# Hybrid conformer and latent-attention trunk on one core: rotary tables made with both parts of the angle side by side, in fewer and wider steps that start sooner

## The chip, the cores and the metric

The kernel runs on one core of one Trainium2 chip. The metric is device time in microseconds (us). A core has TensorE (PE in the profile; its weight loads are PEld), VectorE (DVE), ScalarE (ACT), GpSimd (POOL) and SyncE (SP, which here only issues DMAs). Each engine works through its own list of instructions in order, and waits at an instruction until what it needs is there.

## The reference

Two layers. Each normalises x (256 positions, 2048 channels), multiplies it with one wide input weight, and splits the product into a convolution branch (GLU, causal depthwise convolution of width 31, LayerNorm over channels, SiLU, times a SiLU gate) and an attention branch. Both are projected, merged by sigmoid gates, projected once more and added to x.

```python
def rope_tables(positions, dtype):
    inv_freq = ROPE_THETA ** (-jnp.arange(0, QK_ROPE, 2, dtype=jnp.float32) / QK_ROPE)
    ang = positions.astype(jnp.float32)[..., None] * inv_freq
    cos = jnp.cos(ang)[:, :, None, :].astype(dtype)
    sin = jnp.sin(ang)[:, :, None, :].astype(dtype)
    return cos, sin

def hybrid_layer(...):
    proj = rmsnorm(x, norm_g) @ w_in
    ...
    y_conv = conv_branch(c_a, c_glu, c_gate, conv_w, conv_b, conv_ln_g, conv_ln_b) @ w_proj_conv
    y_mla = mla_branch(q_down, kv_down, k_pe, m_gate, cos, sin, ...) @ w_proj_mla
    y = jax.nn.sigmoid(g_conv) * y_conv + jax.nn.sigmoid(g_mla) * y_mla
    return x + y @ w_out
```

The positions go up to 1279, so an angle is up to some two hundred revolutions. The kernel reduces it to a fraction of one revolution before it takes the sine.

## The kernel before

**Products in parts.** Every fp32 weight is streamed in pieces of 256 rows (two groups of 128) by 512, 384 or 320 columns, numbered in the order of use (raw0, raw1, ...). ScalarE casts a piece to its high part (hi), VectorE subtracts to get the low part (lo), and TensorE adds three products for each group and each half of the positions: twelve matmuls a piece. hi is made three pieces ahead and lo two pieces ahead. A raw buffer (there are five) is free for the next load when both parts are made; there are four hi and three lo buffers, freed by TensorE.

**The order.** It is written out when the program is built, by a small planner. A slot is one weight piece. `product` (with `split_hi` and `split_lo`) lays down the splits and the matmuls of a piece, and `background` then does what is due in that slot: `at_slot(ahead, f, vec, act)` puts a job so many slots ahead and charges its estimated VectorE and ScalarE time to a budget. Each slot gives a budget, less the splits; a debt is carried on, what is left over is not:

```python
            budget[e] = min(budget[e], 0.0) + slot - split_us
```

While VectorE's budget is positive, the planner takes jobs from the list `fill`: the 31 taps of each of the eight convolution blocks, and behind them the LayerNorm, the gates and what makes the input of the projection. A tap is either an addition of what ScalarE scaled (`tap`) or a fused multiply-add (`v_t<-u_t,cst,v_t`). If VectorE's budget is spent elsewhere, the fills move to later slots. Classes around each engine (`InOrder`) then hold every engine to this order.

**The convolution's way to its projection.** In layer 0 the products are, in this order: GLU block 0 (pieces 0 to 7), three blocks of down projections (8 to 31), GLU and attention blocks, gates, and at the end gconv (pieces 244 to 275), pconv (276 to 307), the projection of the convolution branch, and wout. `layernorm` makes the mean (`mu`) and the variance (`var`) with two small matmuls each, which TensorE's order holds between two pieces. Then `apply` normalises each block, ScalarE takes the SiLU, `gated` multiplies by a gate that was parked in DRAM and comes back through POOL's queue as `turned`, and `separated` splits two blocks into the high part ycT0 (ScalarE) and the low part ycT1 (VectorE). There are four such groups; pconv reads the first with pieces 276 and 277, the second with 278 and 279, the third with 280 and 281 and the fourth with 282 and 283. If a group isn't laid down by then, `before_pconv` runs the fills until it is.

**The rotary tables.** `rope_tables` is a generator; each `next` lays down one step. The first loads the inverse frequencies and the positions, the third makes the angle and splits it into a part `ah` with few bits and the rest `al`. The number of revolutions is the angle times 1/(2 pi), which is cut into six pieces of 12 bits. For each piece and each part, `reduce_to` multiplies, rounds by adding and taking away 1.5 x 2^23, and subtracts; the fractions are added up in `turn`. Two more steps make sine and cosine, which the attention of both layers uses, the first time for the key's rotary part some slots behind the down projections.

The first GLU product is read by ScalarE and VectorE (`glu_evac`, the operations `su`) out of two PSUM banks; blocks of products take two pairs of banks in turn, so that down block 1 (from piece 16 on) writes these banks again.

Of the kernel before, what the change touches and what calls it, by code (L numbers as in the profile page):

```python
# [11 lines left out]
F32 = mybir.dt.float32  # L12
F32R = mybir.dt.float32r
I32 = mybir.dt.int32
AF = mybir.ActivationFunctionType
ALU = mybir.AluOpType
# [3 lines left out]
P = 128  # L20
T = 2
# [9 lines left out]
HALF = ROPE // 2  # L31
# [40 lines left out]
def revolution_pieces():  # L72

    from fractions import Fraction

    pi = Fraction(
        "3.14159265358979323846264338327950288419716939937510582097494459230781640628620899"
    )
    rest, out = 1 / (2 * pi), []
    for i in range(REVOLUTION_PIECES):  # L80
        unit = Fraction(1, 1 << (12 * (i + 1)))
        n = int(rest / unit)
        out.append(float(n * unit))
        rest -= n * unit
    return out
# [30 lines left out]
def trunk(ctx: ExitStack, tc: tile.TileContext, xT, x, g_in, pos, win, wuq, wukv, wpc, wpm, wo, cst, rows, invf, out):  # L116
# [19 lines left out]
    pe, vec, act, gps, sp = (InOrder(e) for e in (nc.tensor, nc.vector, nc.scalar, nc.gpsimd, nc.sync))  # L136
# [7 lines left out]
    work = pool("work", 1)  # L144
# [80 lines left out]
    def at_slot(ahead, f, vec=0.0, act=0.0, first=False):  # L225
        steps.insert(0 if first else len(steps), (clock[0] + ahead, (vec, act), f))
# [140 lines left out]
    def stat_of(hi, lo):  # L367
        return lambda k, t: (hi[:, k, t * P : (t + 1) * P], lo[:, k, t * P : (t + 1) * P])
# [120 lines left out]
    def rope_tables():  # L489

        invf_t = const.tile([P, HALF], F32, name="invf_t")
        sp.dma_start(invf_t, invf.partition_broadcast(P))
        pos_t = const.tile([P, T], I32, name="pos_t")
        sp.dma_start(pos_t, pos)
        yield
        yield
        posf = const.tile([P, T], F32, name="posf")
        vec.tensor_copy(posf, pos_t)
        tables = work.tile([P, 6, T, HALF], F32, tag="pr", name="tables")
        ang, ah, al, turn, whole, frac = (tables[:, i] for i in range(6))  # L500
        ah = ah.bitcast(F32R)
        for t in range(T):
            vec.tensor_scalar(ang[:, t, :], invf_t, posf[:, t : t + 1], None, op0=ALU.mult)
        vec.tensor_copy(ah, ang)
        vec.tensor_sub(al, ang, ah.bitcast(F32))
        yield
        big_half = 1.5 * 2.0**23

        def reduce_to(dst, src, scale):

            vec.tensor_scalar(whole, src, scale, big_half, op0=ALU.mult, op1=ALU.add)
            vec.tensor_scalar(whole, whole, -big_half, None, op0=ALU.add)
            vec.scalar_tensor_tensor(dst, src, scale, whole, op0=ALU.mult, op1=ALU.subtract)

        first = True
        for piece in revolution_pieces():
            for a in (ah.bitcast(F32), al):
                reduce_to(turn if first else frac, a, piece)
                if not first:
                    vec.tensor_add(turn, turn, frac)  # L520
                first = False
                yield
        for dst, shift in ((sin2, 0.0), (cos2, 0.25)):
            vec.tensor_scalar(frac, turn, shift, None, op0=ALU.add)
            reduce_to(ang, frac, 1.0)
            for h in range(2):
                act.activation(dst[:, :, h, :], ang, AF.Sin, scale=2.0 * np.pi)
            yield
            yield
# [24 lines left out]
    def first_sums(t, c):  # L554

        xts = []

        def begin():
            for a in (c, c + 1):
                xts.append(wide_p.tile([P, 512], F32, tag="w", name="xres"))  # L560
                sp.dma_start(xts[-1], x[t, :, a * 512 : (a + 1) * 512])

        def end():
            for a, xt in zip((c, c + 1), xts):
                junk = work.tile([P, 512], F32, tag="junk", name="junk")
                act.activation(junk, xt, AF.Square, accum_out=ss_x[:, t, a : a + 1])

        return begin, end


    for l in range(DEPTH):
# [22 lines left out]
        def down_evac(i, t, ps, down=down):  # L594
            at, n = DOWN_BLOCKS[i]
            act.activation(down[:, t, at : at + n], ps, AF.Copy, scale=rinv_x[:, t : t + 1])
# [108 lines left out]
        def rope_squares(b, part_of=part_of):  # L705
            sq = work.tile([P, T, 2, 2, HALF], F32, tag="qa", name="sq")
            act.activation(sq, part_of(b, "qr"), AF.Square)
            late.append(lambda: vec.tensor_reduce(part_of(b, "ss")[:, 2], sq.rearrange("p t a h c -> p t h a c"), axis=AX.XY, op=ALU.add))
# [575 lines left out]
        for kind, i, pl in planned:  # L1284
            if kind == "glu":
                at = EVAC_AT
                if i == 0 and l == 0:
                    at = 6
                    for n, (t, c) in enumerate([(0, 0), (0, 2), (1, 0), (1, 2)]):
                        begin, end = first_sums(t, c)  # L1290
                        at_slot((4, 5, 6, 9)[n], begin)
                        at_slot((9, 9, 10, 12)[n], end, 0.0, 1.5)
                    at_slot(13, sum_x, 2.2)
                elif i == 0:
                    at_slot(8, sum_x, 2.2)
                if i == 0:
                    at_slot(10, load_consts)
                product(pl, uses_h, lambda t, ps, i=i: glu_evac(i, t, ps), at, (0.9, 2.2), tardy=6 if i == 0 and l else None)
            elif kind == "down":
                if l == 0 and i == 0:  # L1300
                    tables = rope_tables()
                    for a in range(20):
                        at_slot(a + (2 if a < 2 else 7), lambda: next(tables, None), 0.0 if a < 2 else 0.95)
                product(pl, uses_h, lambda t, ps, i=i: down_evac(i, t, ps), costs=(0.0, 1.0))
                if i == len(DOWN_BLOCKS) - 1:
                    down_after()
            elif kind == "uq":
                if i == 0:
                    attention_tiles()
                product(pl, of_down(0), lambda t, ps, i=i: uq_evac(i, t, ps), costs=(0.0, 2.5))  # L1310
                if i % 3 == 0:
                    at_slot(EVAC_AT + 1, lambda i=i: rotate_q(4 * (i // 3)), 1.2)
            elif kind == "ukv":
                product(pl, of_down(4), lambda t, ps, i=i: ukv_evac(i, t, ps), costs=(0.0, 2.6))
                attention(i)
                d = 2 * (i // 4)
                if i % 4 < 3:
                    at_slot(3 + d, lambda i=i: rope_squares(i + 1), 0.4, 0.4)
                if i % 4 < 2:
                    at_slot(6 + d, lambda i=i: rotate_q(i + 1), 1.2)  # L1320
                elif i % 4 == 2:
                    at_slot(6 + d, lambda i=i: waiting_in(i + 1), 0.0, 1.6)
                    at_slot(7 + d, lambda i=i: rotate_q(i + 1), 1.2)
                if i == NPAIR - 1:
                    layernorm()
            elif kind == "mgate":
                product(pl, uses_h, lambda t, ps, i=i: mgate_evac(i, t, ps), costs=(0.0, 3.5))
            elif kind == "gmla":
                product(pl, uses_h, lambda t, ps, i=i: gmla_evac(i, t, ps), costs=(0.0, 2.7))
            elif kind == "pmla":  # L1330
                product(pl, stat_of(*keep["o"]), lambda t, ps, i=i: pmla_evac(i, t, ps), costs=(1.25, 0.0))
            elif kind == "gconv":
                product(pl, uses_h, lambda t, ps, i=i: gconv_evac(i, t, ps), costs=(0.0, 3.9))
            elif kind == "cgate":
                product(pl, uses_h, lambda t, ps, i=i: cgate_evac(i, t, ps), costs=(0.0, 2.0))
            elif kind == "pconv":
                while "yc" not in keep:
                    run_fill()
                product(pl, stat_of(*keep["yc"]), lambda t, ps, i=i: pconv_evac(i, t, ps), 0 if i == 3 else EVAC_AT, (2.4, 0.0),
                        before=before_pconv if i == 0 else None)  # L1340
            else:
                wout_begin(i)
                if last_layer and i == 3:
                    wout_end(pl, stat_of(*keep["y"]))
                    continue
                product(pl, stat_of(*keep["y"]), lambda t, ps, i=i, f=wout_evac: f(i, t, ps),
                        0 if i == 3 else EVAC_AT, (1.25, 1.5), tardy=6 if i == 0 else None)
# [108 lines left out]
```

## Time and profile before

| what | value |
|---|---|
| device time, median of 3 runs | 1884.52 us (1883.84 to 1885.91) |
| the profiled execution's own time | 1884.47 us |
| its span in the profile | 1882.7 us |
| mean granted TensorE clock | 0.999 |
| busy TensorE / VectorE / ScalarE / POOL | 99% / 84% / 72% / 26% |
| read from HBM | 399.18 MB |

A row of the chain or of a timeline has the start, the duration, engine, line, operation, output<-inputs and, in brackets, the idle time before it and what ended it. All instructions are issued by one helper, so all have line 127, and the names tell them apart. In a row of waits the numbers are the total, the count and the longest. A row by windows gives the stretch, its length, the busy time of PE, PEld, DVE, ACT and POOL with counts, the granted clock, the DMA share and GB/s. A row of one tile's instructions gives the count, then the shortest, median and longest duration in ns. A row of DMA issues gives the count, the size of one and the median time to landing.

### The profile page before, as it was taken

The numbers are of one execution on the slowest core, as the hardware profiler recorded it, in microseconds if no ns is written. First come the engines' busy times: TensorE is split into PE (matmuls) and PEld (weight loads), VectorE is DVE, ScalarE is ACT, GpSimd is POOL, SyncE is SP. The second block draws the span as 40 slices with busy tenths as digits, with TensorE's granted clock in tenths as the row PEclk, the third lists the DMA queues.
The fourth block names the chain that finished last, engine by engine and source line by source line (L and its number), as shares of the span: only waits on it lengthen the run. The fifth ranks groups of instructions, "written<-read, shape, count | busy, mean of one in ns | idle before, by whom it ended". The sixth has DMA issues, their size and how long they took to land.

```text
span 1882.7 us, 27123 instructions
## 1 busy us (share of the span) xinstructions
PE 1872.1 (99%) x8577; PEld 1571.8 (83%) x8577; DVE 1582.8 (84%) x2452; ACT 1361.7 (72%) x2456; POOL 493.0 (26%) x942
## 2 busy tenths in 40 slices
PE   9999999999999999899999999999999999999999
PEld 8988888888888888788889888888888888888887
DVE  6899998899999988766669899889899999885664
ACT  7678888888887875644557588788889878574442
POOL 1055555532200000022220555555322000001210
PEclk9999999999999999999999999999999999999999
DMA  9688877887765566578876787778877556667775
GB/s 323 218 261 262 267 243 254 270 265 233 243 199 190 194 209 212 172 238 270 298 242 209 261 266 262 247 254 267 269 229 240 199 190 209 202 205 220 245 248 167
DMA packets 138960, 445.05 MB, mean 236 GB/s; under 512 B 23680, under 2 KB 29312, under 8 KB 138816
## 3 DMA queue, kind: packets, MB, share of 16 engines
q1 hardware_dynamic: 105120, 359.89, 58.5%
q0 software_dynamic: 32832, 82.62, 13.6%
q8 instruction: 67, 1.10, 0.3%
q10 hardware_dynamic: 864, 0.80, 0.1%
q14 instruction: 77, 0.63, 0.1%
HBM read 399.18 MB, written 44.04 MB: 235 GB/s over the span
## 4 chain that ended last, share of the span: by engine, by line
PE 99%; DMA 1%; DVE 0%; ACT 0%; issue 0%; SPq 0%; ACTq 0%
PE acc L127 96%; PE s L127 2%; PE o_ps L127 1%; DMA raw<-in_win 0%; DMA gx<-in_g 0%; DVE lo L127 0%; ACT hi L127 0%; ACT v_t L127 0%; PE acc_end L127 0%; DVE turned L127 0%; ACT ycT L127 0%; DVE v_t L127 0%; PE mu L127 0%; PE var L127 0%; DVE xres L127 0%
## 5 line engine op out<-in xcount | busy, mean ns | idle before, releaser
L127 ACT CAST hi<-raw 128x1024 fp32r<-128x1024 f32 (+3 forms) x682 | 699.8, 1031 | 418.4 <-PE acc L127 357.0
L127 DVE TENSOR_TENSOR lo<-raw,hi 128x1024 fp32r<-128x1024 f32 (+3 forms) x682 | 813.8, 1195 | 204.4 <-PE acc L127 149.3
L127 PE MATMUL acc<-hi,hT 128*128 128x512 f32 (+2 forms) x1728 | 419.5, 382 | 0.0
L127 PEld LDWEIGHTS acc<-hi,hT 128*128 128x128 f32 x1728 | 319.6, 188 | 59.1
L127 PE MATMUL acc<-hi,h_hi 128*128 128x512 f32 (+2 forms) x864 | 260.9, 383 | 1.0 <-ACT hi L127 1.0
L127 PE MATMUL acc<-hi,h_lo 128*128 128x512 f32 (+2 forms) x864 | 260.1, 382 | 0.0
L127 ACT ACTIVATE tap<-u_t,cst 128x256 f32<-128x256 f32 x568 | 246.5, 499 | 2.8 <-DVE v_t L127 2.8
L127 PE MATMUL acc<-lo,h_hi 128*128 128x512 f32 (+2 forms) x864 | 229.6, 382 | 0.0
L127 PE MATMUL acc<-lo,hT 128*128 128x512 f32 (+2 forms) x864 | 229.3, 382 | 0.0
L127 DVE TENSOR_TENSOR v_t<-v_t,tap 128x512 f32<-128x512 f32 x284 | 195.3, 688 | 9.5 <-DVE v_t L127 0.5
L127 POOL DMA_DIRECT2D turned<-turn_d x88 | 49.2, 559 | 542.9 <-DVE v_t L127 323.9
L127 PEld LDWEIGHTS acc<-hi,h_lo 128*128 128x128 f32 x864 | 161.1, 188 | 30.3
L127 PEld LDWEIGHTS acc<-lo,h_hi 128*128 128x128 f32 x864 | 160.6, 188 | 30.0
L127 PEld LDWEIGHTS acc<-hi,h_hi 128*128 128x128 f32 x864 | 160.0, 188 | 30.6 <-ACT hi L127 1.9
L127 PEld LDWEIGHTS acc<-lo,hT 128*128 128x128 f32 x864 | 160.6, 188 | 29.9
L127 POOL DMA_DIRECT2D turn_d<-gate x184 | 100.0, 551 | 295.1 <-DVE gate L127 175.3
L127 DVE SCALAR_TENSOR_TENSOR v_t<-u_t,cst,v_t 128x256 f32<-128x256 f32 x392 | 167.8, 479 | 2.4
L127 PE MATMUL acc<-hi,ycT 128*128 128x512 f32 x512 | 129.7, 393 | 5.6 <-ACT ycT L127 5.6
L127 PE MATMUL acc<-hi,oT 128*128 128x512 f32 x512 | 127.8, 389 | 0.0
L127 PE MATMUL acc<-hi,yT 128*128 128x512 f32 x508 | 126.9, 389 | 0.0
L127 PEld LDWEIGHTS acc<-hi,ycT 128*128 128x128 f32 x512 | 96.9, 190 | 26.9 <-ACT ycT L127 6.4
L127 PE MATMUL acc<-hi,qkc 128*128 128x512 f32 x448 | 115.4, 389 | 0.0
(180 smaller groups left out, 2215.7 us busy)
## 6 DMA issues: line engine op xcount, KB each, us to landing
raw<-in_win SPq DMA_DIRECT2D x382, 512.0 KB, 4.2
raw<-in_wpm SPq DMA_DIRECT2D x64, 512.0 KB, 3.3
raw<-in_wpc SPq DMA_DIRECT2D x64, 512.0 KB, 4.3
raw<-in_wo SPq DMA_DIRECT2D x64, 512.0 KB, 4.7
raw<-in_wukv SPq DMA_DIRECT2D x32, 512.0 KB, 4.0
turned<-turn_d POOLq DMA_DIRECT2D x56, 256.0 KB, 4.6
raw<-in_win SPq DMA_DIRECT2D x32, 384.0 KB, 4.7
raw<-in_wuq SPq DMA_DIRECT2D x24, 512.0 KB, 4.3
```

The lines of the kernel that those rows point to most:

```text
L127: ins = getattr(self.engine, name)(*a, **k)
```

## The change

The two parts of the angle stand side by side in one buffer of 9 x 64 columns (it was 6 x 64), as one operand of 128 columns. `reduce_to` works on both at once, so that there are six steps of 128 columns in place of twelve of 64; at the end the two fractions are added. The empty second step is gone. In the schedule the loads come one slot earlier, the arithmetic starts five slots behind the begin of the first down block and not nine, and takes 11 charged steps at 1.1 us, where it was 18 at 0.95.

```diff
         pos_t = const.tile([P, T], I32, name="pos_t")
         sp.dma_start(pos_t, pos)
         yield
-        yield
         posf = const.tile([P, T], F32, name="posf")
         vec.tensor_copy(posf, pos_t)
-        tables = work.tile([P, 6, T, HALF], F32, tag="pr", name="tables")
-        ang, ah, al, turn, whole, frac = (tables[:, i] for i in range(6))
-        ah = ah.bitcast(F32R)
+        tables = work.tile([P, 9, T * HALF], F32, tag="pr", name="tables")
+        ang = tables[:, 0].rearrange("p (t c) -> p t c", t=T)
+        halves, turn, whole, frac = (tables[:, 1 + 2 * i : 3 + 2 * i] for i in range(4))
+        ah, al = halves[:, 0].bitcast(F32R), halves[:, 1]
         for t in range(T):
             vec.tensor_scalar(ang[:, t, :], invf_t, posf[:, t : t + 1], None, op0=ALU.mult)
...
-        def reduce_to(dst, src, scale):
+        def reduce_to(dst, src, scale, whole):
 
             vec.tensor_scalar(whole, src, scale, big_half, op0=ALU.mult, op1=ALU.add)
             vec.tensor_scalar(whole, whole, -big_half, None, op0=ALU.add)
             vec.scalar_tensor_tensor(dst, src, scale, whole, op0=ALU.mult, op1=ALU.subtract)
 
-        first = True
-        for piece in revolution_pieces():
-            for a in (ah.bitcast(F32), al):
-                reduce_to(turn if first else frac, a, piece)
-                if not first:
-                    vec.tensor_add(turn, turn, frac)
-                first = False
-                yield
+        for n, piece in enumerate(revolution_pieces()):
+            reduce_to(frac if n else turn, halves, piece, whole)
+            if n:
+                vec.tensor_add(turn, turn, frac)
+            yield
+        vec.tensor_add(turn[:, 0], turn[:, 0], turn[:, 1])
         for dst, shift in ((sin2, 0.0), (cos2, 0.25)):
-            vec.tensor_scalar(frac, turn, shift, None, op0=ALU.add)
-            reduce_to(ang, frac, 1.0)
+            vec.tensor_scalar(frac[:, 0], turn[:, 0], shift, None, op0=ALU.add)
+            reduce_to(tables[:, 0], frac[:, 0], 1.0, whole[:, 0])
...
                 if l == 0 and i == 0:
                     tables = rope_tables()
-                    for a in range(20):
-                        at_slot(a + (2 if a < 2 else 7), lambda: next(tables, None), 0.0 if a < 2 else 0.95)
+                    for a in range(12):
+                        at_slot(a + 4 if a else 1, lambda: next(tables, None), 1.1 if a else 0.0)
```

On SyncE's queue the loads of `invf_t` and `pos_t` move from behind the loads of raw16, the constants (`cst`) and the gains (`down0`) to ahead of them, right behind the last two `xres` loads. The order of instructions changes at three places of which the prediction speaks.

VectorE in the last pieces of the first down block, behind the last row of the reciprocal root for x. lo15 to lo18 are low parts, acc0_0 and acc0_1 the first GLU product in PSUM. Before:

```order
L127 TENSOR_TENSOR lo15_507<-raw15_379,hi15_475 128x768
L127 SCALAR_TENSOR_TENSOR su_525<-acc0_0_164,rinv_x_149,su_525 128x256
L127 SCALAR_TENSOR_TENSOR su_529<-acc0_1_165,rinv_x_149,su_529 128x256
L127 TENSOR_TENSOR lo16_543<-raw16_409,hi16_509 128x768
L127 TENSOR_TENSOR lo17_561<-raw17_437,hi17_545 128x768
L127 TENSOR_TENSOR lo18_581<-raw18_455,hi18_563 128x768
L127 CAST posf_601<-pos_t_431 128x2
L127 TENSOR_SCALAR tables_603<-invf_t_429,posf_601 128x32 x2
```

Now:

```order
L127 CAST posf_507<-pos_t_407 128x2
L127 TENSOR_SCALAR tables_509<-invf_t_405,posf_507 128x32 x2
L127 CAST tables_509<-tables_509 128x64
L127 TENSOR_TENSOR tables_509<-tables_509 128x64
L127 TENSOR_TENSOR lo15_514<-raw15_379,hi15_475 128x768
L127 TENSOR_SCALAR tables_509<-tables_509 128x128 x2
L127 SCALAR_TENSOR_TENSOR tables_509<-tables_509 128x128
L127 SCALAR_TENSOR_TENSOR su_532<-acc0_0_164,rinv_x_149,su_532 128x256
L127 SCALAR_TENSOR_TENSOR su_536<-acc0_1_165,rinv_x_149,su_536 128x256
L127 TENSOR_TENSOR lo16_553<-raw16_413,hi16_516 128x768
L127 TENSOR_SCALAR tables_509<-tables_509 128x128 x2
L127 SCALAR_TENSOR_TENSOR tables_509<-tables_509 128x128
```

The making of the tables has moved from behind lo18 to ahead of lo15, and a whole step stands behind each of the splits that follow (five full ones, behind lo16 to lo20); the sine's step stands behind lo21, the cosine's behind lo23.

TensorE at the LayerNorm's mean (`mu`) in layer 0; acc252 and acc244 are two of the four blocks of gconv. Before:

```order
L127 MATMUL acc252_1_7393<-hi254_7372,h_lo_152 128x512 x2
L127 MATMUL acc252_0_7392<-lo254_7394,h_hi_151 128x512 x2
L127 MATMUL acc252_1_7393<-lo254_7394,h_hi_151 128x512 x2
L127 MATMUL mu_7451<-parts_7388,ones_101 128x256 x2
L127 MATMUL acc252_0_7392<-hi255_7396,h_hi_151 128x512 x2
```

Now:

```order
L127 MATMUL acc244_1_7218<-hi248_7241,h_lo_152 128x512 x2
L127 MATMUL acc244_0_7217<-lo248_7263,h_hi_151 128x512 x2
L127 MATMUL acc244_1_7218<-lo248_7263,h_hi_151 128x512 x2
L127 MATMUL mu_7317<-parts_7259,ones_101 128x256 x2
L127 MATMUL acc244_0_7217<-hi249_7265,h_hi_151 128x512 x2
```

The mean stands six pieces earlier, and so does the variance (behind piece 258, where it was 264). Nothing else moves on TensorE.

ScalarE at the third and fourth group of ycT0, the input of pconv; v_t are the convolution blocks, sc the gate of gconv. Before:

```order
L127 ACT_TABLE_LOAD
L127 ACTIVATE v_t_6512<-v_t_6512,cst_153 128x256 x2
L127 ACTIVATE v_t_6938<-v_t_6938,cst_153 128x256 x2
L127 CAST hi283_8029<-raw283_7947 128x1024
L127 CAST ycT0_7859<-v_t_5668 128x512
L127 CAST ycT0_7859<-v_t_6116 128x512
L127 CAST hi284_8053<-raw284_7967 128x1024
L127 CAST hi285_8074<-raw285_7985 128x1024
L127 CAST ycT0_7859<-v_t_6512 128x512
L127 CAST ycT0_7859<-v_t_6938 128x512
```

Now:

```order
L127 CAST hi277_7901<-raw277_7816 128x1024
L127 CAST ycT0_7688<-v_t_5486 128x512
L127 CAST ycT0_7688<-v_t_6005 128x512
L127 CAST hi278_7923<-raw278_7834 128x1024
L127 CAST hi279_7946<-raw279_7855 128x1024
L127 ACT_TABLE_LOAD
L127 ACTIVATE sc_7407<-acc268_0_7768,rinv_x_149 128x512
L127 ACTIVATE sc_7407<-acc268_1_7769,rinv_x_149 128x512
L127 CAST ycT0_7688<-v_t_6401 128x512
L127 CAST ycT0_7688<-v_t_6805 128x512
```

Both groups are cast six pieces earlier in the stream of weights. From piece 286 on, the order is as before on every engine, but for one ScalarE table load less at the start of layer 1.

More of the change, by code (lines that the diff above doesn't have):

```diff
@@ L495, in rope_tables @@
         yield
-        yield
         posf = const.tile([P, T], F32, name="posf")
         vec.tensor_copy(posf, pos_t)
-        tables = work.tile([P, 6, T, HALF], F32, tag="pr", name="tables")
-        ang, ah, al, turn, whole, frac = (tables[:, i] for i in range(6))
-        ah = ah.bitcast(F32R)
+        tables = work.tile([P, 9, T * HALF], F32, tag="pr", name="tables")
+        ang = tables[:, 0].rearrange("p (t c) -> p t c", t=T)
+        halves, turn, whole, frac = (tables[:, 1 + 2 * i : 3 + 2 * i] for i in range(4))
+        ah, al = halves[:, 0].bitcast(F32R), halves[:, 1]
         for t in range(T):
             vec.tensor_scalar(ang[:, t, :], invf_t, posf[:, t : t + 1], None, op0=ALU.mult)
-        vec.tensor_copy(ah, ang)
-        vec.tensor_sub(al, ang, ah.bitcast(F32))
+        vec.tensor_copy(ah, tables[:, 0])
+        vec.tensor_sub(al, tables[:, 0], ah.bitcast(F32))
         yield
         big_half = 1.5 * 2.0**23
-        def reduce_to(dst, src, scale):
+        def reduce_to(dst, src, scale, whole):
             vec.tensor_scalar(whole, src, scale, big_half, op0=ALU.mult, op1=ALU.add)
```

## The prediction

> **What bounds the kernel now.** I read the busy shares first, then TensorE's waits, then the chain that ended last, and last TensorE's own rows around the waits.
>
> ```profile
> PE 1872.1 (99%) x8577; PEld 1571.8 (83%) x8577; DVE 1582.8 (84%) x2452; ACT 1361.7 (72%) x2456; POOL 493.0 (26%) x942
> PE acc L127 <- ACT ycT L127: 5.6, 2, 3.2
> PE acc L127 <- ACT hi L127: 1.0, 1, 1.0
> 12.19 164.66 PE acc L127 x804
> ...
> 777.86 0.52 ACT ycT L127
> ...
> 787.60 329.29 PE acc L127 x1524
> ```
>
> TensorE is busy 99% of the span. Work taken from VectorE is worth nothing where TensorE runs without a gap, and from 12.19 us on the chain is TensorE's own, through the whole stage in which the rotary tables are made. After its start TensorE waits twice, 5.6 us in all, both times for ycT, the conv branch's input to its projection in layer 0. Its rows there show the whole price:
>
> ```profile
> 770.42 1.98 PE L127 MATMUL acc<-hi,ycT 128*128 128x512 f32 x8
> 773.14 1.98 PE L127 MATMUL acc<-hi,ycT 128*128 128x512 f32 x8
> 778.43 2.39 PE L127 MATMUL acc<-hi,ycT 128*128 128x512 f32 x8 [2.41 <-ACT ycT L127]
> 781.56 1.98 PE L127 MATMUL acc<-hi,ycT 128*128 128x512 f32 x8
> 787.60 3.54 PE L127 MATMUL acc<-hi,ycT 128*128 128x512 f32 x8 [3.16 <-ACT ycT L127]
> 791.88 1.52 PE L127 MATMUL acc<-hi,ycT 128*128 128x512 f32 x6
> 776.02:778.43 2.41, 0.00 (x1) 0.01 (x1) 2.02 (x5) 2.41 (x5) 0.00 (x0) 1.00 0.64 207
> 784.40:787.60 3.20, 0.04 (x1) 0.00 (x1) 2.63 (x5) 0.94 (x3) 0.00 (x0) 0.96 0.61 200
> 787.60:790.98 3.38, 3.38 (x9) 2.64 (x9) 1.27 (x2) 0.47 (x1) 0.00 (x0) 0.54 0.28 104
> ```
>
> One weight piece (twelve matmuls) takes 773.14 - 770.42 = 2.72 us. The pieces that begin at 773.14, 778.43, 781.56 and 787.60 take 5.29, 3.13, 6.04 and 4.28 us. What each has over 2.72 is 2.57, 0.41, 3.32 and 1.56, together **7.86 us**. The last 1.56 is the clock: in the last windows row the granted clock (third number from the end) is 0.54 over 3.38 us, and 3.38 x 0.46 = 1.55. So this place, 700 us behind the edited code, is the only one with much to gain.
>
> The Trainium skill, page "TensorE: Matmul & The Clock Gate", section on the HAM clock gate, says that the array falls to half clock after an idle window of about 3.4 us and needs a busy one to recover. By that rule a wait of 2.41 us costs only itself and one past about 3 us up to half a window more, an estimate of 1.7 us. The trace agrees, 1.00 before and 0.54 behind the 3.16 us wait, which was enough.
>
> **The change part by part.**
>
> *The table arithmetic.* These rows price it, 64 columns wide now; the others are the nearest wider forms.
>
> ```profile
> L127 DVE TENSOR_SCALAR tables<-tables x30: 181/195/243, 48.5 to 76.1; 128x64 f32<-128x64 f32 x30
> L127 DVE SCALAR_TENSOR_TENSOR tables<-tables x14: 224/226/226, 49.0 to 76.3; 128x64 f32<-128x64 f32 x14
> L127 DVE TENSOR_TENSOR tables<-tables x12: 224/224/225, 47.3 to 71.0; 128x64 f32<-128x64 f32 x12
> 94.30 0.28 DVE L127 SCALAR_TENSOR_TENSOR ccq<-cos,down 128x128 f32<-128x128 f32 x1
> 94.71 0.28 DVE L127 TENSOR_TENSOR ka<-down,ccq 128x128 f32<-128x128 f32 x1
> L127 DVE TENSOR_SCALAR v_t<-u_t,cst x2: 406/406/407, 67.3 to 67.6; 128x256 f32<-128x256 f32 x2
> L127 DVE SCALAR_TENSOR_TENSOR v_t<-u_t,cst,v_t x8: 478/480/485, 83.6 to 105.9; 128x256 f32<-128x256 f32 x8
> ```
>
> Removed are twelve steps: 24 scalar operations at 0.195, 12 fused ones at 0.226 and 11 additions at 0.224, 9.9 us. Added are six: 12 scalar operations of 128 columns, between 0.195 (64 columns) and 0.406 (256), taken as 0.25, as the width lies nearer 64; six fused and five additions at 0.28; one more addition of 64 columns at 0.224. That is 3.0 + 3.1 + 0.2 = 6.3 us (5.6 to 8.2). VectorE is relieved of some 3.6 us, all beside a TensorE without a gap. **Value on the path here: nothing.** With that cover gone it would be those 3.6 us (1.7 to 4.2).
>
> *The steps sooner.* The tables now start ahead of the weight split lo15 and of the two su operations, which read the first GLU product out of its PSUM banks. The next user of these banks is weight piece 16.
>
> ```profile
> 40.59 0.96 DVE L127 TENSOR_TENSOR lo<-raw,hi 128x768 fp32r<-128x768 f32 x1
> 41.47 0.87 DVE L127 SCALAR_TENSOR_TENSOR su<-acc,rinv_x,su 128x256 f32<-128x256 f32 x2
> 46.44 0.16 DVE L127 CAST posf<-pos_t 128x2 f32<-128x2 int32 x1
> 47.28 0.23 DVE L127 TENSOR_TENSOR tables<-tables 128x64 f32<-128x64 f32 x1
> 45.30 0.51 PE L127 MATMUL acc<-hi,h_hi 128*128 128x384 f32 x2
> 46.69 0.85 PE L127 MATMUL acc<-lo,h_hi 128*128 128x384 f32 x4
> 59.86 0.51 PE L127 MATMUL acc<-hi,h_hi 128*128 128x384 f32 x2
> ```
>
> su ends at 42.34 now. The head of the tables (46.44 to 47.51, 1.07 us) and the first step (two scalar and one fused operation, 0.78, with 0.1 between them) come ahead of it: 44.3, against the 45.30 at which piece 16 starts. At the 256-column price the step is 1.39 and su ends at 44.8, still in time. Then every piece of 768 elements has a split (0.88 from start to start) and a step of 0.25 x 2 + 0.28 x 2 + 0.1 = 1.16: 2.04 us, against 2.08 of TensorE for a piece (45.30 to 59.86 is seven). lo16 is ready at 45.2 and read at 46.69; that 1.5 us of slack stays. At the upper price (1.87 for a step) VectorE loses 0.67 a piece: lo18 would be 0.4 us late, and lo21, the last one with a full step ahead of it, **2.4 us late**. I take nothing, and keep 2.4 for the range. This stage has no gain to give, only that loss.
>
> ```profile
> 30.30 0.86 SPq L127 DMA_DIRECT2D xres<-in_x  x2
> invf_t<-in_invf SPq DMA_DIRECT2D x1, 16.0 KB, 6.8
> pos_t<-in_pos SPq DMA_DIRECT2D x1, 1.0 KB, 5.8
> 37.63 1.77 ACT L127 CAST hi<-raw 128x768 fp32r<-128x768 f32 x2
> 71.42 1.28 ACT L127 ACT_TABLE_LOAD   x1
> 50.50 0.57 POOL L127 DMA_DIRECT2D turned<-turn_d  x1 [0.91 <-DMA turn_d<-su]
> turned<-turn_d POOLq DMA_DIRECT2D x32, 128.0 KB, 4.3
> ```
>
> The two loads that feed the tables move on SyncE's queue ahead of raw16, cst and the gains' rows, to right behind the xres pair: issued by about 32, landed by 38, while VectorE turns to them at 40.59. They push raw16 back by some 0.8 us; it is cast at 38.5, second in the row at 37.63, and TensorE wants it at 45.30. POOL's turns of su start 2 us later and so land at 50.5 + 2 + 4.3 = 56.8; VectorE's transposes of them stand behind lo23, which waits for hi23 until about 58. ScalarE's sine table load (1.28) and the sines go from 71.42 to ahead of hi23. That cast waits for them until about 57 and ends near 58, against 59.86, where TensorE starts piece 23. Nothing on the path.
>
> *What the planner does with it.* The table steps are charged 11 x 1.1 = 12.1 us of VectorE where it was 18 x 0.95 = 17.1, and they stand in slots where no convolution tap is ready, whose unused budget lapses. So the taps start at once when their input is back. The order of work shows the result: the LayerNorm's mean goes from behind weight piece 254 to behind 248, its variance from 264 to 258. Six pieces are 6 x 2.72 = 16.3 us of head start. The third of the four ycT groups is now cast behind hi277, the fourth behind hi279, not behind 283 and 285. Is that enough?
>
> ```profile
> 734.81 0.40 PE L127 MATMUL var<-parts,ones 128*128 128x256 f32 x2
> 1647.66 0.40 PE L127 MATMUL var<-parts,ones 128*128 128x256 f32 x2
> 1693.17 1.14 ACT L127 CAST ycT<-v_t 128x512 fp32r<-128x512 f32 x2 [1.40 <-DVE v_t L127]
> 1679.10:1701.00 21.90, 21.90 (x99) 18.12 (x98) 18.66 (x26) 14.68 (x19) 0.00 (x0) 1.00 0.58 186
> ```
>
> In layer 1 the fourth group ends 1694.3 - 1647.66 = 46.6 us behind the variance, and TensorE runs through (21.90 busy of 21.90). In layer 0 the variance moves to 734.81 - 16.32 = 718.5; even at the slow pace of now (788.1 - 734.81 = 53.3) the fourth group is there at 771.8. Without waits TensorE wants it at 773.14 + 3 x 2.72 = 781.3, so 9.5 us are spare. Both waits go, and with the second the half clock.
>
> **Sum:** 1884.47 (the profiled execution; its span is 1882.7) - 7.86 = 1876.61. That execution lies 0.05 under the median of the runs shown, so **1876.6**. Layer 1's order is unchanged, but for one ScalarE table load less.
>
> **The rivals.**
>
> *One wait stays.* The fourth group hangs on the gates' turn through DRAM and on a cast behind two table loads. If only the first wait goes (2.57 + 0.41), the time is 1884.47 - 2.98 = 1881.5. Against it stand the 9.5 us spare. Chance 0.06.
>
> *The change doesn't reach the waits.* If the gates or the weight stream set ycT, both waits stay: 1884.5. For it: the relief is only 3.6 us. Against it: the order moves by six pieces whatever the durations, and layer 1 streams the same weights at 186 GB/s without a gap. Chance 0.05.
>
> *Slower: posf waits for its load at the head of VectorE's queue.* Behind it stand lo15, su and all later splits, and TensorE waits for su's banks. From a landing at 40.59 + 1.0 = 41.6 on, each microsecond costs one, and 1.6 more once the gap passes 3 us; the gain is eaten at 41.6 + 7.86 - 1.6 = 47.9. A landing at 53 gives 1876.6 + 11.4 + 1.6 = 1889.6. The loads took 6.8 and 5.8 us; from an issue at 32 they would have to take 16 for a loss. Chance 0.03.
>
> **How the numbers follow.** The forecast has 0.85, and 0.01 is left over. The range goes from the fastest run shown less the gain and half the spread of the three (1883.84 - 7.86 - 1.0 = 1875.0) to the slowest less the gain plus the 2.4 (1885.91 - 7.86 + 2.4 = 1880.5). What can be told from no change is 0.2%, 3.8 us, so faster means under 1880.75. With part of the first rival, faster has 0.88, same 0.09, slower 0.03.
>
> **What would show it.** Right: no wait of TensorE for ycT; the granted clock at 1.00 everywhere between 700 and 800; the variance near 718.5; 12 scalar operations of 128 columns on the tables, near 0.25 each; a span near 1874.8. Wrong: a gap of TensorE between 44 and 60, behind su or a late lo (tables too dear there, or a late load), or a remaining wait for ycT, which names the first or second rival.

## The result, and the profile after

The changed kernel takes **1875.72 us** (median of 6 runs, 1875.29 to 1876.36). The kernel before, run beside it, takes 1884.87 (6 runs, 1883.41 to 1885.91). The ratio is 0.9952, with an interval of 0.9939 to 0.9965. The forecast was 1876.6. The profiled execution of the change took 1876.14 us, with a span of 1874.3.

The busy shares and the waits of TensorE after the change:

```profile
PE 1869.3 (100%) x8577; PEld 1571.1 (84%) x8577; DVE 1577.5 (84%) x2428; ACT 1362.0 (73%) x2458; POOL 491.8 (26%) x942
PE acc L127 <- ACT hi L127: 0.8, 1, 0.8
```

VectorE has 5.3 us less to do (1582.8 to 1577.5). The tables account for 3.7 of it (12.22 us of VectorE before, 8.53 now); the total of profiles with the same arithmetic differs by up to 3.2 us (1582.8 before, 1579.6 in e4), so the rest is within that scatter. Of the rows of waits for data one is left, and it is the start. The row for ycT is gone. These are TensorE's matmuls at the place of the two waits, in the changed kernel's timeline. Here and below only the matmuls at the head of a piece are shown, and rows between them are left out:

```profile
772.68 1.98 PE L127 MATMUL acc<-hi,ycT 128*128 128x512 f32 x8
...
775.40 1.98 PE L127 MATMUL acc<-hi,ycT 128*128 128x512 f32 x8
...
780.84 1.98 PE L127 MATMUL acc<-hi,ycT 128*128 128x512 f32 x8
```

The same stretch by windows:

```profile
764.90:792.00 27.10, 27.10 (x122) 22.42 (x121) 15.79 (x17) 14.31 (x16) 2.62 (x5) 1.00 0.64 197
```

The piece that reads the third group is the one at 775.40, the one that reads the fourth is at 780.84. Every piece starts 2.72 us behind the one before (the two shown are two pieces, 5.44 us, apart), and the stretch of 27.10 us is busy throughout, at a granted clock of 1.00. The two groups are now cast long ahead of that (ScalarE):

```profile
759.37 1.14 ACT L127 CAST ycT<-v_t 128x512 fp32r<-128x512 f32 x2
...
767.84 1.14 ACT L127 CAST ycT<-v_t 128x512 fp32r<-128x512 f32 x2
```

The fourth group ends at 769.0, 11.9 us before TensorE wants it.

The chain of waits has TensorE alone from 11.72 us to the end, where it began at 12.19 before:

```profile
11.72 164.67 PE acc L127 x804
...
718.20 0.23 PE var L127 x2
```

The two profiled executions differ by 1884.47 - 1876.14 = 8.33 us: the 7.86 of the prediction, and 0.47 from a start of TensorE that happened to come sooner. The order of work is the same up to there, and in the nine profiles whose chain begins at that start it lies between 11.38 (e8) and 12.19.

The medians differ by more, 9.15 us. The granted clock shows why. For the 28 runs of the kernel before that were made beside the experiments, it is one of two values:

| kernel | mean granted clock | runs | median us |
|---|---|---|---|
| before | 0.999 | 8 | 1883.65 |
| before | 0.998 | 20 | 1885.33 |
| the change | 1.000 | 6 | 1875.72 |

The profiled execution of before has 0.999. The next section shows what the others lose, and the last one why.

### The profile page after: what moved, and what is told of

The parts are those of the page before. It is cut to its first block, busy times and chain, and to the rows that moved or that the text cites. A ratio compares the mean times of both kernels' runs of the same rounds, so it can differ in the third digit from the quotient of the medians.

```text
span 1874.3 us, 27110 instructions
## 1 busy us (share of the span) xinstructions
PE 1869.3 (100%) x8577; PEld 1571.1 (84%) x8577; DVE 1577.5 (84%) x2428; ACT 1362.0 (73%) x2458; POOL 491.8 (26%) x942
## 3 DMA queue, kind: packets, MB, share of 16 engines
q0 software_dynamic: 32832, 82.62, 13.7%
## 4 chain that ended last, share of the span: by engine, by line
PE 99%; DMA 1%; ACT 0%; DVE 0%; SPq 0%; issue 0%
PE acc L127 96%; PE s L127 2%; PE o_ps L127 1%; DMA raw<-in_win 0%; DMA gx<-in_g 0%; PE acc_end L127 0%; ACT hi L127 0%; PE mu L127 0%; PE var L127 0%; DVE xres L127 0%; SPq L127 0%
## 5 line engine op out<-in xcount | busy, mean ns | idle before, releaser
L127 PEld LDWEIGHTS acc<-hi,oT 128*128 128x128 f32 x512 | 96.1, 188 | 19.9
```

What stands on the lines that cost most here:

```text
L127: ins = getattr(self.engine, name)(*a, **k)
```

## The experiments

Four theories are told apart. **A**: all of the gain is the order of work behind pconv, which comes from the planner's slots and charges. **B**: it is VectorE's relief. **C**: the tables, sooner or wider, bring something in themselves. **D** came up on the way, with the charges below: it isn't the amount of head start that counts, but the place of the last two ycT groups in the order. This table shows where these stand in the kernels that were run (mean: the piece behind whose matmuls it stands on TensorE; groups: the piece behind whose hi ScalarE casts them):

| kernel | mean behind piece | the four groups behind hi of piece |
|---|---|---|
| before, e1, e3 | 254 | 276, 278, 283, 285 |
| after, e2, e4, e8 | 248 | 268, 271, 277, 279 |
| e5 | 252 | 272, 276, 279, 282 |
| e6 | 256 | 276, 279, 283, 285 |
| e7 | 245 | 265, 269, 272, 275 |
| e9 | 254 | 276, 278, 281, 283 |
| e10 | 253 | 273, 277, 280, 283 |

### Arithmetic and plan, crossed

**e1_wide_old_plan**: the change's wide arithmetic, laid down at the slots and charges of before. Each wide step is followed by an empty one, so that the count is the same. Against the change:

```diff
         yield
+        yield
         posf = const.tile([P, T], F32, name="posf")
...
             yield
+            yield
         vec.tensor_add(turn[:, 0], turn[:, 0], turn[:, 1])
...
-                    for a in range(12):
-                        at_slot(a + 4 if a else 1, lambda: next(tables, None), 1.1 if a else 0.0)
+                    for a in range(20):
+                        at_slot(a + (2 if a < 2 else 7), lambda: next(tables, None), 0.0 if a < 2 else 0.95)
```

> The six wide steps, laid down in the slots and with the charges of the kernel before (every second step is empty), so that all else stands in the order of before: the mean behind piece 254. Theory A (the order's head start of six pieces is all of the gain): both waits for ycT stay, 1884.9 us, within 2 of the kernel before, though VectorE works some 3.6 us less. Rival B (VectorE's relief is what counts): 1881.3 or less.

Measured: 1884.72 us (10 runs, 1883.42 to 1886.59), beside 1884.94 for the kernel before (19 runs); ratio 1.0001, interval 0.9991 to 1.001. The busy shares and TensorE's waits in e1:

```profile
PE 1872.9 (99%) x8577; PEld 1572.5 (83%) x8577; DVE 1579.1 (84%) x2429; ACT 1361.5 (72%) x2456; POOL 491.4 (26%) x942
PE acc L127 <- ACT ycT L127: 5.6, 2, 3.2
```

VectorE's relief is there (1582.8 to 1579.1: 3.7 us, where the prediction has 3.6), and so are both waits. B falls: the relief alone is worth nothing that ten runs can tell.

**e2_narrow_new_plan**: the reverse, twelve narrow steps laid down two to a slot, at the slots and charges of the change. Against the kernel before, the main one of its edits (the other two take out the empty second step and put in the change's schedule):

```diff
         for piece in revolution_pieces():
             for a in (ah.bitcast(F32), al):
                 reduce_to(turn if first else frac, a, piece)
                 if not first:
                     vec.tensor_add(turn, turn, frac)
                 first = False
-                yield
+            yield
```

> The twelve narrow steps, two to a slot, laid down in the slots and with the charges of the change, so that all else stands in its order: the mean behind piece 248. A: no wait for ycT. A pair of narrow steps takes 1.86 us and a split 0.87, against 2.08 for a piece, so VectorE falls behind by 0.65 a piece and lo18 to lo21 come late, by 2.3 us in the end: 1875.7 + 2.3 = 1878.0 (1876 to 1879). B: no gain, 1884.9.

Measured: 1877.65 us (4 runs, 1877.23 to 1878.07), ratio 0.9961, interval 0.9946 to 0.9976. The waits for ycT are gone, and TensorE now waits while the tables are made. The low parts on VectorE in e2's timeline, and the matmuls that read them on TensorE:

```profile
52.28 0.95 DVE L127 TENSOR_TENSOR lo<-raw,hi 128x768 fp32r<-128x768 f32 x1
54.86 0.95 DVE L127 TENSOR_TENSOR lo<-raw,hi 128x768 fp32r<-128x768 f32 x1
```

```profile
53.28 0.97 PE L127 MATMUL acc<-lo,h_hi 128*128 128x384 f32 x4 [0.20 <-DVE lo L127]
...
63.40 0.45 PE L127 MATMUL acc<-hi,h_hi 128*128 128x320 f32 x2
```

The stretch of the tables in e2, by windows:

```profile
40.00:64.00 24.00, 23.31 (x131) 22.03 (x130) 22.09 (x77) 11.84 (x21) 5.67 (x10) 1.00 0.56 173
```

A split and two narrow steps take VectorE 2.58 us a piece, where TensorE needs 2.08. So TensorE goes at VectorE's pace for some pieces: it starts the first piece of the next block, the first matmul of 320 columns, at 63.40. In the change that matmul starts at 61.49:

```profile
61.49 0.45 PE L127 MATMUL acc<-hi,h_hi 128*128 128x320 f32 x2
```

That is 1.91 us, and 1877.65 - 1875.72 = 1.93. Only 0.69 of it shows as idle time (23.31 busy of 24.00); the rest lies in matmuls that fill the time until their operand is there (0.97 for 0.85). C falls as a source of gain; but the width is what makes the sooner place free.

### The plan alone

**e3_charge_180**: the change with one number altered.

```diff
-                        at_slot(a + 4 if a else 1, lambda: next(tables, None), 1.1 if a else 0.0)
+                        at_slot(a + 4 if a else 1, lambda: next(tables, None), 1.8 if a else 0.0)
```

> The change as it is, but each table step is charged 1.8 us and not 1.1, which puts the mean back behind piece 254; tables as wide and as soon as in the change. A: both waits are back, 1884.9. Rival C (tables made sooner, and wide, are themselves the gain): 1875.7.

Measured: 1885.29 us (10 runs, 1883.26 to 1885.64), ratio 1.0, interval 0.9991 to 1.001. The whole gain is gone, with the same instructions for the tables at the same early place. TensorE's rows around the waits in e3's timeline, with the rows between left out:

```profile
771.92 1.98 PE L127 MATMUL acc<-hi,ycT 128*128 128x512 f32 x8
...
777.21 3.04 PE L127 MATMUL acc<-hi,ycT 128*128 128x512 f32 x8 [2.41 <-ACT ycT L127]
...
781.75 2.17 PE L127 MATMUL acc<-hi,ycT 128*128 128x512 f32 x8
...
787.99 3.48 PE L127 MATMUL acc<-hi,ycT 128*128 128x512 f32 x8 [3.16 <-ACT ycT L127]
...
792.69 1.55 PE L127 MATMUL acc<-hi,ycT 128*128 128x512 f32 x6
```

The two stretches behind the waits, by windows:

```profile
777.21:780.25 3.04, 3.04 (x9) 2.18 (x10) 1.27 (x2) 0.46 (x1) 0.00 (x0) 0.74 0.47 170
787.99:791.47 3.48, 3.48 (x9) 2.47 (x10) 1.27 (x2) 0.47 (x1) 0.00 (x0) 0.64 0.21 85
```

The waits are as long as before, 2.41 and 3.16. But here the clock falls behind both, to 0.74 and 0.64. Taken piece by piece over the 2.72 us that one takes, the place costs 2.57 + 1.82 + 3.52 + 1.98 = 9.89 us, against 7.86 in the profiled execution of before; 1885.29 - 1875.72 is 9.57. So the same two waits have two prices, by whether the first of them takes the clock down. The 20 runs of before at 0.998 and the 8 at 0.999 are 1.7 us apart, and the first of the pieces behind a wait differs by 1.82 - 0.41 = 1.4.

**e4_charge_30_narrow**: the kernel before with one number altered.

```diff
-                        at_slot(a + (2 if a < 2 else 7), lambda: next(tables, None), 0.0 if a < 2 else 0.95)
+                        at_slot(a + (2 if a < 2 else 7), lambda: next(tables, None), 0.0 if a < 2 else 0.3)
```

> The kernel before with one number changed: each of its 18 table steps is charged 0.3 us and not 0.95, which puts the mean behind piece 248 as in the change. Twelve narrow steps in their old slots, loads as before. A: 1875.7, if VectorE, which really spends 0.9 on each, doesn't fall behind by more than its splits are ahead; up to 2 more if it does. B and C: 1884.9.

Measured: 1876.65 us (4 runs, 1876.11 to 1877.44), ratio 0.9956, interval 0.9941 to 0.9971. There is no wait for ycT, though the narrow arithmetic stands where it stood. One small wait is new on TensorE. The planner now takes the tables for cheaper than they are and puts more beside them:

```profile
75.32 0.56 PE L127 MATMUL acc<-lo,h_hi 128*128 128x320 f32 x2 [0.33 <-DVE lo L127]
```

The pair e3 and e4 settles A against B and C: one charge takes all of the gain away from the new tables, and another brings 8.3 us of it to the old ones.

### How much head start it takes

**e5_charge_155, e6_charge_220, e7_charge_0**: the change with 1.55, 2.2 and 0 in place of 1.1, one run each, beside 1885.78 for the kernel before.

> The change with its table steps charged 1.55 us: the mean behind piece 252, two pieces sooner than before (5.4 us) and four later than in the change. A: the fourth group of ycT, which TensorE got at 787.6 in the kernel before, comes at 782.2 or a little sooner, and is wanted at 781.3: at most 0.9 us of a wait is left, 1875.7 to 1876.6. The gain is then no ramp over the six pieces, but is all had within the first two or three.

> The change with its table steps charged 2.2 us: the mean behind piece 256, two pieces later than before. A: both waits grow, the second by 5.4 us at most, 1888 to 1891, with the tables as wide and as soon as in the change. B and C: 1875.7.

> The change with its table steps charged nothing: the mean behind piece 245, three pieces sooner still. A: nothing is left to gain, TensorE has no gap there: 1875.7, within 1. If more head start went on paying: 1870 or so.

Measured: 1876.74, 1889.46 and 1876.18 us. With 1.55 the head start is two pieces in place of six, and no wait for ycT is left. The fourth group's cast, on ScalarE in e5, comes as soon as VectorE has made its input:

```profile
774.71 1.14 ACT L127 CAST ycT<-v_t 128x512 fp32r<-128x512 f32 x2 [1.40 <-DVE v_t L127]
```

With 0 the mean comes three pieces sooner than in the change, and brings nothing more. With 2.2 it is two pieces later than before, and dearer. TensorE in e6:

```profile
772.59 1.98 PE L127 MATMUL acc<-hi,ycT 128*128 128x512 f32 x8
...
779.64 3.78 PE L127 MATMUL acc<-hi,ycT 128*128 128x512 f32 x8 [4.17 <-ACT ycT L127]
...
784.93 2.23 PE L127 MATMUL acc<-hi,ycT 128*128 128x512 f32 x8
...
792.65 3.48 PE L127 MATMUL acc<-hi,ycT 128*128 128x512 f32 x8 [4.58 <-ACT ycT L127]
...
796.89 1.53 PE L127 MATMUL acc<-hi,ycT 128*128 128x512 f32 x6
```

Over 2.72 a piece this is 4.33 + 2.57 + 5.00 + 1.52 = 13.4 us, and 1889.46 - 1875.72 = 13.7. Two pieces of delay are 5.4 us, but the waits grow by no more than 4.17 - 2.41 and 4.58 - 3.16. The last two groups are already at the latest place that they can have, behind hi283 and hi285. What the waits have grown by is work for them that now stands later too: ScalarE's table load and SiLUs stand behind hi283 and not ahead of it, and on VectorE both products with the gate of the fourth group stand behind lo284, where one did.

This gives theory D. Each engine works in order, and a split takes a buffer that TensorE has to free. There are four hi and three lo buffers, so that hi283 and lo282 wait for piece 279, and hi285 and lo284 for piece 281. What stands behind these splits is later still. Yet the third group is wanted by piece 280 and the fourth by piece 282, the very next ones. So a group that is laid down only when its piece forces it is late by its own making, and a group that stands some pieces ahead is not.

Of the two kinds of buffers, it is the lo buffers that count in the kernel before. VectorE's last product with the gate (v_t<-turned,v_t) stands right behind lo282 for the third group and right behind lo284 for the fourth. TensorE is through with piece 279 at 776.02 and with piece 281 at 784.40:

```profile
776.11 1.23 DVE L127 TENSOR_TENSOR lo<-raw,hi 128x1024 fp32r<-128x1024 f32 x1
777.26 0.76 DVE L127 TENSOR_TENSOR v_t<-turned,v_t 128x256 f32<-128x256 f32 x2
...
784.53 1.22 DVE L127 TENSOR_TENSOR lo<-raw,hi 128x1024 fp32r<-128x1024 f32 x1
...
786.41 0.76 DVE L127 TENSOR_TENSOR v_t<-turned,v_t 128x256 f32<-128x256 f32 x2
```

```profile
786.93 1.14 ACT L127 CAST ycT<-v_t 128x512 fp32r<-128x512 f32 x2 [2.26 <-DVE v_t L127]
```

Both splits start 0.1 us after TensorE is through, and the casts follow the products. At the fourth group ScalarE is done with hi285 and stands 2.26 us for VectorE. At the third ScalarE is as late as VectorE: behind hi282, which waits for piece 278, it works without a pause through a table load, four SiLUs and hi283 up to the cast. The second wait needs no first one: it counts from the end of piece 281, whenever that is.

**e9_groups_two_slots_sooner**: a test of D alone. The kernel before, its tables and charges untouched, with the groups forced two slots ahead of the piece that reads them.

```diff
         def before_pconv(j, keep=keep):
-            c = j * KS // 4
+            c = min(j + 2, 7) * KS // 4
```

> The kernel before with one line changed: the planner is made to lay down a group of ycT two pieces ahead of the piece that reads it, and not with that piece. Tables, charges, mean (behind 254) and variance (behind 264) are those of before; only the third and fourth group move, from behind hi283 and hi285 to behind hi281 and hi283. Theory D (what costs is the place of the two groups in the order: a cast behind hi283 can't run before TensorE is through with piece 279, whose buffer hi283 takes, and piece 280 already wants the group): the third group comes by 773, the fourth by 782.2 or sooner, wanted at 775.9 and 781.3: 1875.7 to 1877.5. Theory A as I had it (the whole convolution must run six pieces sooner): the work of both groups is only crowded into earlier slots and comes no sooner, 1884.9, or splits come late beside it.

Measured: 1878.17 us (5 runs, 1877.43 to 1878.49), beside 1885.34 (8 runs); ratio 0.9964, interval 0.995 to 0.9978. The mean stands where it stood, behind piece 254. The waits of TensorE for ycT are down from 5.6 us to 1.04:

```profile
771.77 1.98 PE L127 MATMUL acc<-hi,ycT 128*128 128x512 f32 x8
...
774.94 2.40 PE L127 MATMUL acc<-hi,ycT 128*128 128x512 f32 x8 [0.29 <-ACT ycT L127]
...
778.11 1.98 PE L127 MATMUL acc<-hi,ycT 128*128 128x512 f32 x8
...
781.75 2.38 PE L127 MATMUL acc<-hi,ycT 128*128 128x512 f32 x8 [0.75 <-ACT ycT L127]
...
784.87 1.52 PE L127 MATMUL acc<-hi,ycT 128*128 128x512 f32 x6
```

The fourth group's cast on ScalarE in e9:

```profile
781.08 1.14 ACT L127 CAST ycT<-v_t 128x512 fp32r<-128x512 f32 x2 [3.76 <-DVE v_t L127]
```

What is left is 0.45 + 0.45 + 0.92 + 0.40 = 2.2 us; 1878.17 - 1875.72 = 2.45. On VectorE the last product of the fourth group now stands behind lo282 and not lo284, and that of the third behind lo280, so neither waits for the piece just ahead of the group's reader. What ends the fourth group's wait is still VectorE's v_t, for which ScalarE stands 3.76 us. So the place of the groups is worth some 7 us of the gain, and the rest needs the work on VectorE sooner too. The result lies 0.7 above the range that was expected of it, for that reason.

**e10_charge_170**: the change with 1.7, one tenth under the 1.8 of e3. The head start is one piece.

> The change with its table steps charged 1.7 us, which puts the mean behind piece 253, one piece (2.7 us) sooner than before, and the third and fourth group behind hi280 and hi283. If the gain goes with the head start: a wait of 2.57 us shrinks to nothing and one of 4.9 to some 2.2, so that 2 or 3 us are left, 1878 to 1879. D: both groups stand where TensorE doesn't want them yet, and the whole gain is there: 1875.7 to 1877.

Measured: 1875.67 us (4 runs, 1875.63 to 1876.6), ratio 0.9952, interval 0.9937 to 0.9966, so the whole gain. TensorE and the fourth group's cast on ScalarE in e10:

```profile
774.98 1.98 PE L127 MATMUL acc<-hi,ycT 128*128 128x512 f32 x8
...
780.41 1.98 PE L127 MATMUL acc<-hi,ycT 128*128 128x512 f32 x8
```

```profile
777.35 1.15 ACT L127 CAST ycT<-v_t 128x512 fp32r<-128x512 f32 x2 [2.03 <-DVE v_t L127]
```

The fourth group ends at 778.5, 1.9 us ahead of the piece at 780.41. Between 1.7 and 1.8 there is a step of 9.6 us and no slope. With 1.7 the groups are cast behind hi280 and hi283, not 283 and 285, and the fourth group's last product stands behind lo281, not lo284. That is D.

### The load ahead of VectorE's queue

**e8_loads_late**: the change with the two loads of the tables four slots later. It tests the third rival.

```diff
-                        at_slot(a + 4 if a else 1, lambda: next(tables, None), 1.1 if a else 0.0)
+                        at_slot(a + 4 if a else 5, lambda: next(tables, None), 1.1 if a else 0.0)
```

> The change with the two loads of the tables laid down four slots later, in the slot of their use: they go out behind raw19, near 38 us, and land between 43.9 and 45.3, where VectorE turns to them at 40.1. My third rival: VectorE stands still for 4 to 5 us with lo15 and su behind it, TensorE, which wants lo15 at 43.8 and su's banks at 44.8, waits 2.8 to 4.0 us, and up to 1.6 more if the clock falls to half behind it: 1878.5 to 1881.3. If the slack is larger than I worked out: 1875.7.

Measured: 1876.75 us, one run. VectorE stands at posf, TensorE loses half a microsecond behind it, and the rows of the DMA issues give the time to landing, all of e8:

```profile
42.09 0.17 DVE L127 CAST posf<-pos_t 128x2 f32<-128x2 int32 x1 [2.25 <-DMA pos_t<-in_pos]
```

```profile
44.10 0.62 PE L127 MATMUL acc<-lo,h_hi 128*128 128x384 f32 x2 [0.47 <-DVE lo L127]
```

```profile
invf_t<-in_invf SPq DMA_DIRECT2D x1, 16.0 KB, 4.1
pos_t<-in_pos SPq DMA_DIRECT2D x1, 1.0 KB, 3.8
```

The expectation missed on two counts. The loads took 4.1 and 3.8 us to land and not some 6. And 2.25 us of standing cost 0.47, so the slack here is 1.8 us and not the 1.0 that the prediction gave. The first to wait is the reader of lo15, not the next user of su's banks. The rival's mechanism exists; its threshold was set too low.

## Why the prediction was right, point by point

**The bound and the place of the gain: right.** Both waits for ycT went with the half clock behind them, and no wait took their place.

**The size: right for the profiled execution, short for the median.** 8.33 us between the profiled executions is 7.86 and the sooner start. The median gained 9.15, since the 7.86 was measured in an execution in which the first wait left the clock up. The prediction noted that the execution lay 0.05 from the median of three runs and left it there. The clock of more runs would have shown two kinds, with the profiled one in the smaller; that it was this kind was chance. This is the term that was mis-sized: 7.86 for one kind, up to 9.89 (e3) for the other.

**Table arithmetic worth nothing: right** (e1). The terms, from the groups of the changed kernel (shortest, median and longest duration in ns):

```profile
L127 DVE TENSOR_SCALAR tables<-tables x18: 187/219/228, 42.0 to 57.6; 128x128 f32<-128x128 f32 x12, 128x64 f32<-128x64 f32 x6
L127 DVE SCALAR_TENSOR_TENSOR tables<-tables x8: 225/292/293, 42.5 to 57.9; 128x128 f32<-128x128 f32 x6, 128x64 f32<-128x64 f32 x2
```

A scalar operation of 128 columns takes about 0.22 where 0.25 was taken, and a fused one 0.292 where it was 0.28. So the steps cost slightly less than forecast, and the choice of a value near the 64-column row was the right one.

**The early steps in their cover: right, with a little more room.** The rows of su and the first low parts on VectorE in the changed kernel:

```profile
42.70 0.87 DVE L127 SCALAR_TENSOR_TENSOR su<-acc,rinv_x,su 128x256 f32<-128x256 f32 x2
...
45.40 0.95 DVE L127 TENSOR_TENSOR lo<-raw,hi 128x768 fp32r<-128x768 f32 x1
47.32 0.95 DVE L127 TENSOR_TENSOR lo<-raw,hi 128x768 fp32r<-128x768 f32 x1
```

su ends at 43.57 (forecast 44.3; 0.5 of that is TensorE's sooner start, and piece 16 starts at 44.85, so the slack is 1.3 us where 1.0 was forecast). A split with its step takes 1.92 us (forecast 2.04) against 2.08 for TensorE. The upper bound of 2.4 us was the right kind of loss: e2 has it, 1.9 us, with narrow steps at the same place. The two loads of the tables, issued at 30.84 and 31.32, took 5.4 and 5.1 us and landed ahead of the 38 of the forecast.

**The planner: right in its result, incomplete in its reason.** The variance is at 718.20 (forecast 718.5), and the fourth group ended 2.8 us sooner than the latest time given. But the argument compared six pieces of head start with the need, as if each piece were worth 2.72 us. One piece is enough (e10), and two slots of place bring most of it with no head start at all (e9). The prediction knew where the two casts stood, behind 283 and 285, and passed over what stands ahead of the groups' last steps: splits that can't be written until TensorE has come to the piece right before the reader.

**The rivals.** That one of the two waits stays alone was seen in no kernel here: they came as a pair and went as a pair. The one whose waits the change doesn't reach fell with e3 against e10. The load at the head of VectorE's queue is real and small (e8).

## What to carry to other kernels

Where engines work in order, read a late operation together with the instruction ahead of it, and ask which buffer that one waits for: a job that stands behind a split whose buffer is freed by the piece just ahead of the job's reader can't be in time, whatever its inputs. A planner's charge is a lever on work 700 us away, and it acts in steps: vary it alone before crediting the edit that came with it. And price a wait from several executions when the clock behind it can go either way.

## What the runs showed of the hardware

The same wait of TensorE has taken the clock down in one execution and left it up in another. In the piece behind a gap of 2.41 us the mean granted clock was 1.00 in the profiled execution of before, 0.74 in e3 and 0.54 in e1. The windows rows show what decides it. A fall lasts 3.41 us at half clock, or twice that (e6), and the falls of an execution stand on a grid of 3.41 us: those of e3 begin at 778.70 and 788.94, three times 3.41 apart. What counts is TensorE's busy time (the second number) in the stretch of that grid ahead of the fall. Two stretches of before with a gap in them, and the one behind the second:

```profile
777.08:780.50 3.42, 2.07 (x8) 1.43 (x9) 2.23 (x5) 1.81 (x3) 0.00 (x0) 1.00 0.64 207
783.91:787.32 3.41, 0.53 (x3) 0.10 (x1) 3.10 (x6) 1.15 (x2) 0.00 (x0) 1.00 0.62 187
787.32:790.74 3.42, 3.14 (x7) 2.46 (x8) 1.29 (x2) 0.75 (x2) 0.00 (x0) 0.50 0.32 120
```

And a stretch of e3 with the same gap of 2.41, and the one behind it:

```profile
775.28:778.70 3.42, 1.49 (x5) 0.97 (x6) 2.81 (x5) 2.39 (x4) 0.00 (x0) 1.00 0.68 248
778.70:782.11 3.41, 3.41 (x9) 2.67 (x8) 0.12 (x1) 1.04 (x1) 0.00 (x0) 0.50 0.04 14
```

In before a border of the grid, at 777.08, cuts the first gap in two. Neither part is longer than 3.42 - 2.07 = 1.35 us, and the clock stays up. In e3 3.42 - 1.49 = 1.93 us of the gap lie in one stretch, and the clock falls at its end. In all the profiles here, stretches at full clock with up to 1.35 us idle were followed by full clock, and those with 1.93 or more by half; nothing between was met. So the length of a gap doesn't tell alone, as the prediction took it: where it lies on the grid counts too. One fall costs up to 3.41 / 2 = 1.7 us, which is what lies between the two kinds of runs of before, and 1.7 in 1884 us is 0.0009 of the mean clock, so that 0.999 fits one fall and 0.998 two. The Trainium skill, page "TensorE: Matmul & The Clock Gate", section on the HAM clock gate, says that the activity window is free-running, so that the same kernel can meet it at another phase in each run. The two kinds of runs agree with that, and so does the length of a fall with the page's window of about 3.4 us; that the whole window must be idle doesn't agree, since 1.93 was enough.
